# Attention stage: low halves of weights and queries, and the rotation's sum, moved from GpSimd to VectorE

## The chip, the cores and the metric

The kernel runs on one core of one Trainium2 chip. The core has a matrix engine (TensorE, PE in the profile; PEld is its weight load), three engines for elementwise work (VectorE or DVE, ScalarE or ACT, GpSimd or POOL), and a queue (SyncE, SP) that issues this kernel's DMAs. The metric is the device time of one execution in microseconds. Each engine takes its instructions strictly in the order of its own queue; semaphores between engines say when an instruction may start.

## The reference, cut to what matters

Two residual layers, 1024 tokens by 1024 channels, float32. The first has a recurrent mixer, the second windowed attention; each is followed by a squared-ReLU MLP. The attention mixer is:

```python
def rope(t, cos, sin):
    half = t.shape[-1] // 2
    t1, t2 = t[..., :half], t[..., half:]
    return jnp.concatenate([t1 * cos - t2 * sin, t2 * cos + t1 * sin], axis=-1)

def window_attention(u, w_qkv, sinks, w_o, cos, sin, band_mask):
    ...
    qkv = u @ w_qkv
    q, k, v = jnp.split(qkv, ...)          # 16 query heads, 4 key/value heads of 64
    q = rope(q..., cos, sin)
    k = rope(k..., cos, sin)
    ...                                    # blocks of 128 queries, keys of 3 blocks
    sc = einsum('bnqhgd,bnkhd->bnhgqk', qb, kb) * (HEAD_DIM ** -0.5)
    sc = where(band_mask, sc, -inf)
    p = softmax(concatenate([sc, sink], axis=-1), axis=-1)[..., :-1]
    o = einsum('bnhgqk,bnkhd->bnqhgd', p, vb)
    return o.reshape(bsz, s, N_Q_HEADS * HEAD_DIM) @ w_o
```

## The kernel before, in words

Products are made in a reduced float format (F32R). To keep accuracy each operand is split: the high half is a copy rounded to F32R by ACT (`split`, L85), the low half is the rest, source minus high half (L86). A product of two split operands takes three matmuls: high by high, high by low, low by high.

The attention stage works on slabs of 128 columns of `w_qkv`, each in two halves of 512 tokens. `load_split` brings a slab's weights from HBM into `raw`, and splits them into `w1hl`. `proj` (L116) makes the 24 matmuls of one half into PSUM tile `m`. The slab's `evac` then rotates: ACT copies PSUM to `qf` (L1130), four DMAs in SP's queue write the swapped 32-row groups to `rot` (L1132), DVE multiplies `qf` by the cosines in place (L1133), POOL multiplies `rot` by the sines (L1134), and their sum goes to `qf` (L1135). For queries (`put_q`) ACT copies 64 rows as the high half into one half of the tile `qst` (L1161), and the low half goes into the other 64 rows (L1162), so that one matmul contracts both. For keys (`put_k`) ACT makes `kh` (L1147), DVE `kl` (L1148), and DMAs copy both to the other 64 rows (L1149, L1150). Values (`do_v`) are transposed and split (L1178, L1179).

A unit is one of 4 key/value heads by one of 8 blocks of 128 queries: 32 units. For each of its 4 query heads it makes scores (PE L1208 on `kh`, L1209 on `kl`), adds the mask and takes the minimum of the negated scores (DVE L1210, tiles `sm` and `nm`), takes exponentials and their sum (ACT L1216), and the reciprocal (DVE L1217). Per block of keys it transposes (PE L1222), splits the probabilities into `ph` (ACT L85) and `pl` (DVE L86), and multiplies by the values (PE L1227, L1228). A transposed denominator (PE L1231), a sum (ACT L1233, DVE L1234) and a product (DVE L1237) end it. POOL also copies the sink's column into each `sm` (L1204).

The order in which slabs (K, Q, V, with group, slab and half) and units (U) are recorded is the string `ATT_ORDER`:

```python
ATT_ORDER = ("K00 Q010 Q000 K01 Q011 Q001 V00 !U00 !U01 !U02 V01 !U03 Q100 !U06 Q110 !U04 "
             "!U07 U05 Q101 !U11 !U12 !U10 !U13 Q111 Q200 U14 Q210 !U17 !U15 U16 Q201 Q211 "
             "K10 K11 V10 !U20 !U21 !U22 V11 !U23 Q300 Q310 !U24 !U26 !U27 !U32 !U33 !U30 "
             "!U25 Q301 Q311 !U31 !U34 !U35 !U36 U37")
```

This is not the queues' final order. A scheduler places all recorded instructions from its own estimate of what each takes on its engine, so an instruction that changes its engine can change the order on every engine. The slabs' matmuls, and near the end the first half of the output projection (L216), are what PE does between the steps of the units.

`mm_state['pool_lo']` is set when the first unit is recorded, and cleared at the stage's end. While it is set, a slab that is loaded has its weights' low half made by POOL, and the rotation's sum is POOL's too. The low halves of the queries are POOL's for the groups 1 to 3 (`G if g else V`). What the recurrent mixer, the MLPs and the output projections split is DVE's in any case.

Of the kernel before, what the change touches and what calls it, by code (L numbers as in the profile page):

```python
# [13 lines left out]
ALU = mybir.AluOpType  # L14
# [37 lines left out]
def trunk_kernel(ctx, tc, x, norm_g, rec_w_in, rec_conv_w, rec_conv_b, rg_w_r, rg_b_r, rg_w_i,  # L52
# [3 lines left out]
    V, A, G, T, Y = nc.vector, nc.scalar, nc.gpsimd, nc.tensor, nc.sync  # L56
# [11 lines left out]
    mm_state = {"n": 0, "att": False}  # L68
# [15 lines left out]
    def split(hi, lo, src, eng=None):  # L84
        A.activation(hi, src, AF.Copy)  # L85
        (eng or V).tensor_tensor(lo, src, hi, op=ALU.subtract)  # L86

    def load_split(dram_view, shape, pool, tag, bufs):
        raw = wp.tile(shape, F32, tag="raw", name="raw")
        Y.dma_start(raw, dram_view)  # L90
        both = pool.tile(shape[:1] + [2] + shape[1:], F32R, tag=tag, name=tag + "hl", bufs=bufs)
        hi, lo = both[:, 0], both[:, 1]
        split(hi, lo, raw, G if mm_state.get('pool_lo') else None)
        return hi, lo

    ahead = {}
# [1 line left out]
    def load_w1(w, c0):  # L98
        if (id(w.tensor), c0, w.offset) in ahead:
            return ahead.pop((id(w.tensor), c0, w.offset))  # L100
        return load_split(w[:, c0:c0 + P].rearrange("(k p) c -> p k c", p=P), [P, KT, P], wp, "w1", 3)
# [174 lines left out]
    def out_proj(ys, w, h_src, h_dst, layer, nxt, pre):  # L276
# [7 lines left out]
        def load_wo(k, pool, tag, bufs):  # L284
            return load_split(w[k * P:(k + 1) * P, :], [P, D], pool, tag, bufs)
# [820 lines left out]
    def attention(xt, a):  # L1106
        w_qkv = att_w_qkv[a]
        ys = [yp.tile([P, S], F32, tag="y", name=f"y{i}") for i in range(KT)]
        with phase("att") as pool:
# [13 lines left out]
            def h512(name, bufs=2):  # L1123
                return pool.tile([P, 512], F32, tag=name, name=name, bufs=bufs)

            def slab(c0, put):
                def evac(hf, o):
                    sl = slice(hf * 512, hf * 512 + 512)
                    qf, rot = h512("qf"), h512("rot", 2)
                    A.activation(qf, o, AF.Copy)  # L1130
                    for i, j in ((0, 1), (1, 0), (2, 3), (3, 2)):
                        Y.dma_start(rot[32 * i:32 * i + 32, :], qf[32 * j:32 * j + 32, :])  # L1132
                    V.tensor_tensor(qf, qf, cos[:, sl], op=ALU.mult)  # L1133
                    G.tensor_tensor(rot, rot, sin[:, sl], op=ALU.mult)  # L1134
                    (G if mm_state.get('pool_lo') else V).tensor_tensor(qf, qf, rot, op=ALU.add)  # L1135
                    put(hf, sl, qf)
                return load_w1(w_qkv, c0), evac

# [17 lines left out]
            def put_q(g, e0):  # L1156
                def f(hf, sl, r):
                    for e in range(2):
                        src, oth = (lo64, hi64) if e == 0 else (hi64, lo64)
                        t = qst[g, hf, e0 + e]  # L1160
                        A.activation(t[src, :], r[src, :], AF.Copy)  # L1161
                        (G if g else V).tensor_tensor(t[oth, :], r[src, :], t[src, :], op=ALU.subtract)  # L1162
                return f

            def do_v(pair):
# [85 lines left out]
            for st in ATT_ORDER.split():  # L1251
                if "U" in st:
                    g, n = int(st[-2]), int(st[-1])
# [101 lines left out]
```

## Time and profile before

| | |
|---|---|
| time, median of 3 runs | 2212.37 us (2211.07 to 2213.91) |
| profiled execution, its own time | 2211.91 us |
| its span, first to last instruction | 2210.2 us |
| mean granted clock of TensorE | 0.995 |
| instructions of POOL | 132, 168.8 us busy |
| of them, sums of the rotation on POOL (L1135) | 14, 19.7 us |
| low halves of queries on POOL (L1162) | 24, 31.5 us |
| low halves of weights on POOL (L86) | 8, 19.1 us |

Rows of instructions have: start and duration in us (or count, busy us and mean ns for a group), engine, source line, operation, output<-inputs, shapes; in square brackets, or behind the second bar, the idle time of the engine before them and what ended it. In the table of windows PE's busy time comes from modelled ends of pipelined matmuls. A granted clock of 1.00 is TensorE's full speed.

### The profile page before, as it was taken

The page shows a single profiled execution, that of the slowest core. Times are in us where ns is not written, and L with a number is a line of the kernel's source. Part 1 is how long each engine was busy: PE and PEld are TensorE (multiplying, and loading weights), DVE is VectorE, ACT ScalarE, POOL GpSimd, SP SyncE. Part 2 cuts the span into 40 slices and gives each one's busy share as a digit, 9 for nine tenths or more (in the row PEclk, how much of TensorE's full clock was granted, in tenths as well). Part 3 has the DMA queues.
Part 4 walks back from the last instruction along what each step waited for, and adds up shares of the span by engine and source line. Part 5 has one row for each costly group of instructions (what it writes and reads, how often), then busy time and mean ns, then how long its engine had stood idle before and what let it go on. Part 6 is the DMA issues. An engine that isn't in the chain of part 4 may idle for free.

```text
span 2210.2 us, 28051 instructions
## 1 busy us (share of the span) xinstructions
PE 2155.5 (98%) x10392; PEld 1779.2 (80%) x10392; DVE 1662.6 (75%) x2783; ACT 1145.7 (52%) x1798; POOL 168.8 (8%) x132
## 2 busy tenths in 40 slices
PE   8999999999999999999999999999999999999998
PEld 7878888787788888888888777777788888888886
DVE  6697867848976665778887775886896666578888
ACT  6576545635655446333444765775654455533332
POOL 0000000002000000000022245311200000000000
PEclk9999999999999999999999999999999999999999
DMA  5211111134444436444344112104354444634433
GB/s 144 62 34 58 29 30 39 39 124 138 143 156 154 152 135 254 153 149 157 115 143 129 44 38 63 39 25 140 128 170 156 148 151 159 228 133 152 157 122 131
DMA packets 180762, 260.88 MB, mean 118 GB/s; under 512 B 17040, under 2 KB 98960, under 8 KB 180624
## 3 DMA queue, kind: packets, MB, share of 16 engines
q1 hardware_dynamic: 180624, 259.07, 35.4%
q8 instruction: 82, 1.34, 0.3%
q14 instruction: 56, 0.46, 0.1%
HBM read 180.92 MB, written 70.78 MB: 114 GB/s over the span
## 4 chain that ended last, share of the span: by engine, by line
PE 78%; DVE 12%; ACT 6%; issue 2%; DMA 1%; POOL 1%; SPq 0%; DVEq 0%; ACTq 0%; POOLq 0%
PE m L437 15%; PE m L701 13%; PE m L116 12%; PE aux L437 10%; PE aux L701 10%; PE m L216 9%; PE aux L1227 1%; PE aux L1222 1%; DVE hb L267 1%; PE m L1208 1%; ACT sm L1216 1%; PE m L1209 1%; DVE acc L185 1%; PE aux L1049 1%; DVE w1hl L86 1%
## 5 line engine op out<-in xcount | busy, mean ns | idle before, releaser
L116 PE MATMUL m<-xh,w1hl 128*128 128x512 f32 (+1 forms) x1472 | 426.0, 369 | 0.2 <-ACT qf L1130 0.2
L116 PEld LDWEIGHTS m<-xh,w1hl 128*128 128x128 f32 x1472 | 266.3, 191 | 38.5 <-ACT qf L1130 0.4
L116 PE MATMUL m<-xl,w1hl 128*128 128x512 f32 (+1 forms) x736 | 271.5, 369 | 0.5 <-DVE xl L205 0.5
L86 DVE TENSOR_TENSOR w1hl<-raw,w1hl 128x1024 fp32r<-128x1024 f32 x110 | 133.8, 1219 | 89.7 <-ACT w1hl L85 89.4
L437 PE MATMUL m<-xh,ws 128*128 128x512 f32 x512 | 168.8, 392 | 4.1 <-ACT ws L85 3.0
L437 PE MATMUL aux<-xh,w1hl 128*128 128x512 f32 x512 | 168.7, 391 | 1.7 <-ACT u L453 1.3
L437 PE MATMUL m<-xh,w1hl 128*128 128x512 f32 x512 | 167.1, 389 | 0.0
L624 ACT ACTIVATE hidh<-hidl 128x1536 fp32r<-128x1536 f32 (+1 forms) x56 | 89.4, 1596 | 147.3 <-DMA hidl<-hs 147.3
L701 PE MATMUL m<-w2h,hidh 128*128 128x512 f32 x416 | 161.9, 389 | 0.0
L701 PE MATMUL m<-w2h,hidl 128*128 128x512 f32 x416 | 161.9, 389 | 0.0
L701 PE MATMUL m<-w2l,hidh 128*128 128x512 f32 x416 | 161.8, 389 | 0.0
L116 PEld LDWEIGHTS m<-xl,w1hl 128*128 128x128 f32 x736 | 140.8, 191 | 19.2 <-DVE xl L205 0.8
L265 POOL TENSOR_TENSOR mg<-acc,g 128x1024 f32<-128x1024 f32 x24 | 61.2, 2551 | 1162.6 <-DVE acc L610 608.0
L625 DVE TENSOR_TENSOR hidl<-hidl,hidh 128x1536 fp32r<-128x1536 f32 (+1 forms) x56 | 105.9, 1890 | 56.4 <-ACT hidh L624 56.4
L85 ACT ACTIVATE w1hl<-raw 128x1024 fp32r<-128x1024 f32 x118 | 124.1, 1055 | 33.9 <-DMA raw<-in_mlp_w_dram 9.6
L85 ACT ACTIVATE w2h<-b 128x1536 fp32r<-128x1536 f32 (+1 forms) x48 | 76.7, 1598 | 102.1 <-PE m L701 50.0
L85 ACT ACTIVATE ws<-s 128x512 fp32r<-128x512 f32 x88 | 55.3, 631 | 140.6 <-PE m L437 78.9
L701 PE MATMUL aux<-w2h,hidl 128*128 128x512 f32 x312 | 121.4, 389 | 0.0
L701 PE MATMUL aux<-w2h,hidh 128*128 128x512 f32 x312 | 121.4, 389 | 0.0
L701 PE MATMUL aux<-w2l,hidh 128*128 128x512 f32 x312 | 121.4, 389 | 0.0
L437 PEld LDWEIGHTS m<-xh,ws 128*128 128x128 f32 x512 | 95.8, 188 | 28.1 <-ACT ws L85 5.5
L437 PEld LDWEIGHTS aux<-xh,w1hl 128*128 128x128 f32 x512 | 96.1, 188 | 22.8 <-ACT u L453 2.3
(304 smaller groups left out, 4982.7 us busy)
## 6 DMA issues: line engine op xcount, KB each, us to landing
raw<-in_mlp_w_dram SPq DMA_DIRECT2D x32, 1024.0 KB, 5.6
hidl<-hs SPq DMA_DIRECT2D x42, 768.0 KB, 4.5
hs<-hid SPq DMA_DIRECT2D x104, 256.0 KB, 2.0
b<-in_mlp_w_dram SPq DMA_DIRECT2D x24, 768.0 KB, 4.8
raw<-in_rec_w_in_dram SPq DMA_DIRECT2D x28, 512.0 KB, 3.7
hidl<-hs SPq DMA_DIRECT2D x14, 1024.0 KB, 5.7
hs<-u SPq DMA_DIRECT2D x52, 256.0 KB, 2.0
hres<-hb SPq DMA_DIRECT2D x24, 512.0 KB, 2.7
```

What stands on the lines that cost most here:

```text
L85: A.activation(hi, src, AF.Copy)
L86: (eng or V).tensor_tensor(lo, src, hi, op=ALU.subtract)
L116: T.matmul(o[:, c0:c0 + nw], a[:, k, :], b[k // 4][half][:, k % 4, c0:c0 + nw], start=(n == 0), stop=(n == 3 * KT - 1))
L185: V.scalar_tensor_tensor(hg, hb, r[:, 0:1], g, op0=ALU.mult, op1=ALU.mult)
L216: T.matmul(o, p_[:, b * P:(b + 1) * P], q_[:, c * 512:(c + 1) * 512], start=(n == 0), stop=(n == n3 - 1))
L265: G.tensor_tensor(mg, m, g_post, op=ALU.mult)
L267: V.scalar_tensor_tensor(hb, mg, r[:, 0:1], hb, op0=ALU.mult, op1=ALU.add)
L437: T.matmul(o, a[:, k, :], b[:, k, :], start=(first and n == 0), stop=(n == 11), skip_group_check=not first)
L624: A.activation(h, f32(l), AF.Copy)
L625: V.tensor_tensor(l, f32(l), h, op=ALU.subtract)
L701: T.matmul(o, a_[:, j, sl], b_[:, j, :], start=(not more and n == 0), stop=(n == last), skip_group_check=more)
L1049: T.matmul(o, a_, b_, start=(i == 0), stop=(i == len(terms) - 1))
```

## The change

In three places DVE takes what POOL did: the low half of weights that are loaded while the units run, the sum that ends a rotation, and the low halves of the queries of groups 1 to 3. POOL keeps the sines' product (L1134) and the sinks' copies (L1204). The flag `pool_lo` is still set but no longer read.

```diff
@@ load_split
-        split(hi, lo, raw, G if mm_state.get('pool_lo') else None)
+        split(hi, lo, raw)
@@ slab, evac
                     V.tensor_tensor(qf, qf, cos[:, sl], op=ALU.mult)
                     G.tensor_tensor(rot, rot, sin[:, sl], op=ALU.mult)
-                    (G if mm_state.get('pool_lo') else V).tensor_tensor(qf, qf, rot, op=ALU.add)
+                    V.tensor_tensor(qf, qf, rot, op=ALU.add)
@@ put_q
                         A.activation(t[src, :], r[src, :], AF.Copy)
-                        (G if g else V).tensor_tensor(t[oth, :], r[src, :], t[src, :], op=ALU.subtract)
+                        V.tensor_tensor(t[oth, :], r[src, :], t[src, :], op=ALU.subtract)
```

The queues of PE, DVE, ACT and SP are reordered by it from the first unit to the end of the stage. Three places follow, as differences (- stood before, + stands now).

DVE's queue at the first unit, U00. `qst` are the queries of group 0, `m_10069` to `m_10081` the scores of its four heads:

```order
 L1133 TENSOR_TENSOR qf<-qf,cos 128x512
 L1135 TENSOR_TENSOR qf<-qf,rot 128x512
+L86 TENSOR_TENSOR w1hl<-raw,w1hl 128x1024
 L1162 TENSOR_TENSOR qst<-qf,qst 64x512 x2
 L1210 ISA sm,nm<-m_10069,mask,nsink 128x256
 L1210 ISA nm 128x1
+L1210 ISA sm,nm<-m_10073,mask,nsink 128x256
+L1210 ISA nm 128x1
```

A weight split now stands ahead of the two low halves that the first scores need.

POOL's queue where the last slabs of group 2 (`qf_11489`, `qf_11528`) and the second pair of keys (`qf_11576`, `qf_11619`) are rotated:

```order
-L1162 TENSOR_TENSOR qst_11461<-qf_11489,qst_11461 64x512
-L86 TENSOR_TENSOR w1hl_11991<-raw_11989,w1hl_11991 128x1024
 L1134 TENSOR_TENSOR rot_11529<-rot_11529,sin_9610 128x512
-L1135 TENSOR_TENSOR qf_11528<-qf_11528,rot_11529 128x512
-L1162 TENSOR_TENSOR qst_11462<-qf_11528,qst_11462 64x512
-L1162 TENSOR_TENSOR qst_11463<-qf_11528,qst_11463 64x512
 L1134 TENSOR_TENSOR rot_11577<-rot_11577,sin_9610 128x512
-L1135 TENSOR_TENSOR qf_11576<-qf_11576,rot_11577 128x512
-L86 TENSOR_TENSOR w1hl_12039<-raw_12037,w1hl_12039 128x1024
 L1134 TENSOR_TENSOR rot_11620<-rot_11620,sin_9610 128x512
-L1135 TENSOR_TENSOR qf_11619<-qf_11619,rot_11620 128x512
```

Between the sines' products nothing is left on POOL there.

DVE's queue at the same place, to the first score of the second pair's first unit:

```order
+L1162 TENSOR_TENSOR qst_11462<-qf_11528,qst_11462 64x512
+L1162 TENSOR_TENSOR qst_11463<-qf_11528,qst_11463 64x512
 L1133 TENSOR_TENSOR qf_11576<-qf_11576,cos_9609 128x512
+L1135 TENSOR_TENSOR qf_11576<-qf_11576,rot_11577 128x512
+L86 TENSOR_TENSOR w1hl_12039<-raw_12037,w1hl_12039 128x1024
 L1148 TENSOR_TENSOR kl_11543<-qf_11576,kh_11542 64x512
 L1148 TENSOR_TENSOR kl_11545<-qf_11576,kh_11544 64x512
+L1179 TENSOR_TENSOR vs_11637<-aux_11671,vs_11637 128x4x64
 L1210 ISA sm_11681,nm_11680<-m1_11683,mask_9613,nsink_9622 128x256
```

The keys' sum and a weight split now stand between their cosine product and their low halves.

## The prediction

> **What bounds the kernel now.** I read the head of the page first, then the chain that ended last, then the attention stage by windows, groups and waits.
>
> ```profile
> span 2210.2 us, 28051 instructions
> PE 2155.5 (98%) x10392; PEld 1779.2 (80%) x10392; DVE 1662.6 (75%) x2783; ACT 1145.7 (52%) x1798; POOL 168.8 (8%) x132
> ...
> 667.16 10.88 PE m L437 x48
> ```
>
> TensorE (PE) is the bound. The third row is one link of the chain: 48 matmuls of 512 columns in 10.88 us, 0.227 us each, with nothing between. Only what makes PE wait, or slows it, can move the end. The diff acts only after the first attention unit is recorded, so I look at the stretch from the attention stage's first products to the end of its last unit, about 1182 to 1510 us:
>
> ```profile
> core 0: us, PE busy (x) PEld busy (x) DVE busy (x) ACT busy (x) POOL busy (x), PEclk, DMA share, GB/s
> 1182.00:1510.00 328.00, 313.64 (x1705) 252.10 (x1704) 242.66 (x604) 213.25 (x482) 106.31 (x100) 0.98 0.17 47
> 1206.00:1212.00 6.00, 4.53 (x24) 4.27 (x25) 5.55 (x11) 3.30 (x8) 2.09 (x2) 0.72 0.66 184
> 1364.00:1376.00 12.00, 8.52 (x35) 6.88 (x35) 7.02 (x18) 5.84 (x17) 3.18 (x2) 0.72 0.36 99
> ```
>
> The columns are the busy times, then the granted clock. PE stands idle 328 - 313.64 = 14.4 us. In two places the clock falls (0.72 over 6 us and over 12 us), worth 0.28 x 6 = 1.7 and 0.28 x 12 = 3.4 us. Together 19.5 us: no gain can be larger, since the PE's own work does not change. Here are the first of the two places, and the second:
>
> ```profile
> 1204.04 2.37 POOL L86 TENSOR_TENSOR w1hl<-raw,w1hl 128x1024 fp32r<-128x1024 f32 x1 [0.82 <-ACT w1hl L85]
> 1204.64 4.00 DVE L1162 TENSOR_TENSOR qst<-qf,qst 64x512 fp32r<-64x512 f32 x2 [0.70 <-ACT qst L1161]
> 1206.36 1.73 POOL L1134 TENSOR_TENSOR rot<-rot,sin 128x512 f32<-128x512 f32 x1
> 1207.05 0.37 PE L1208 MATMUL m<-kh,qst 128*128 128x256 f32 x1 [1.80 <-POOL w1hl L86]
> 1208.69 0.58 PE L1208 MATMUL m<-kh,qst 128*128 128x256 f32 x1 [0.42 <-DVE qst L1162]
> ...
> 1356.55 1.99 DMA rot<-qf
> ...
> 1360.92 1.30 POOL L1134 TENSOR_TENSOR rot<-rot,sin 128x512 f32<-128x512 f32 x1
> 1362.30 1.29 POOL L1135 TENSOR_TENSOR qf<-qf,rot 128x512 f32<-128x512 f32 x1
> 1363.55 2.36 POOL L86 TENSOR_TENSOR w1hl<-raw,w1hl 128x1024 fp32r<-128x1024 f32 x1
> ...
> 1364.29 2.17 DVE kl L1148
> ...
> 1366.62 0.47 PE L1208 MATMUL m<-kh,qst 128*128 128x256 f32 x2 [2.18 <-DMA kh<-kh]
> 1368.85 0.77 PE L1209 MATMUL m<-kl,qst 128*128 128x256 f32 x2 [1.29 <-DMA kl<-kl]
> ```
>
> At 1204 two low halves of queries on DVE take 4.00 us instead of about 1.4, because they lie beside POOL's weight split and then beside its sines' product, and the first scores wait for them. At 1364 the keys of the second pair are late: their rotation stood in POOL's queue behind another slab's work, and their low half on DVE took 2.17 us beside POOL's split of 1363.55. Each place cost the wait, and the lower clock behind it.
>
> **The change, part by part.** The groups that it moves, and their like on DVE:
>
> ```profile
> L1162 POOL TENSOR_TENSOR qst<-qf,qst 64x512 fp32r<-64x512 f32 x24 | 31.5, 1311 | 18.6 <-ACT qst L1161 17.8
> L1135 POOL TENSOR_TENSOR qf<-qf,rot 128x512 f32<-128x512 f32 x14 | 19.7, 1410 | 11.7 <-DVE qf L1133 11.3
> L86 POOL TENSOR_TENSOR w1hl<-raw,w1hl 128x1024 fp32r<-128x1024 f32 x8 | 19.1, 2382 | 28.5 <-DVE y L1237 14.6 <-ACT w1hl L85 13.8
> ...
> L86 DVE TENSOR_TENSOR pl<-aux,ph 128x512 fp32r<-128x512 f32 x88 | 60.0, 687 | 18.5 <-ACT ph L85 18.1
> L1133 DVE TENSOR_TENSOR qf<-qf,cos 128x512 f32<-128x512 f32 x20 | 18.3, 914 | 10.5 <-POOL w1hl L86 5.2 <-DMA rot<-qf 5.0
> L1162 DVE TENSOR_TENSOR qst<-qf,qst 64x512 fp32r<-64x512 f32 x8 | 8.1, 1010 | 1.6 <-ACT qst L1161 1.4
> L86 DVE TENSOR_TENSOR w1hl<-raw,w1hl 128x1024 fp32r<-128x1024 f32 x4 | 4.9, 1226 | 0.5 <-ACT w1hl L85 0.3
> ```
>
> POOL loses 24 + 14 + 8 instructions, 70.3 us. DVE gets the same 46: 24 x 0.687 + 14 x 0.687 + 8 x 1.226 = 35.9 us. It sheds some stretching: its low halves of queries mean 1010 against the 687 of the same 512 columns read from PSUM, 8 x 0.32 = 2.6 us, and part of L1133's 20 x 0.23 = 4.5 us. So DVE goes from 242.7 to about 274 of 328 us, 74 to 83%. No DMA is added or dropped, PE and ACT do the same work. No instruction of POOL is now a link between a slab's cosine product and its finished query, except the sines' product (L1134), which stays.
>
> (1) The first scores, 1204 to 1210. In the new DVE queue the weight split (1.23) stands ahead of the two low halves: from 1204.04, where POOL's began, it lasts to 1205.3, then come 2 x 0.69 and one sines' product of 1.29 that can slip between: 1206.7 to 1208.0 against 1204.64 + 4.00 = 1208.64 now. PE has five more projection matmuls of 256 columns ahead of the first score, at half of 0.227 each 0.6 us of cover. Saved: 0.6 to 2.0 us of wait, and 0 to 1.7 of clock. I take 1.8.
>
> (2) The keys, 1356 to 1376. The transfer landed at 1356.55 + 1.99 = 1358.54, the sines' product began at 1360.92. With POOL's queue empty it begins 2.4 us sooner, the sum is 0.6 shorter, and the low half 1.5; the weight split that the new queue puts ahead of it costs about 0.6 back. The high half comes 3.0 us sooner (wait now 2.18), the low half 3.9 (the two waits 3.47). Bounds: all of 3.47 + 3.4 = 6.9, or nothing, if the transfers from `qf` land late. I take 5.5.
>
> (3) Waits in the rest of the stage that POOL ends:
>
> ```profile
> ACT qst L1161 <- POOL qf L1135: 8.1, 7, 2.5
> ...
> PE m L1208 <- POOL qst L1162: 1.0, 2, 0.6
> ...
> 1300.00:1310.00 10.00, 8.59 (x44) 6.08 (x43) 6.09 (x13) 6.49 (x14) 8.06 (x6) 1.00 0.21 61
> 1380.00:1390.00 10.00, 9.33 (x49) 7.93 (x50) 9.31 (x27) 6.87 (x16) 0.19 (x1) 1.00 0.23 54
> 1410.00:1420.00 10.00, 9.89 (x57) 7.96 (x56) 9.08 (x24) 8.32 (x17) 5.78 (x5) 1.00 0.10 26
> 1450.00:1460.00 10.00, 7.94 (x42) 5.35 (x41) 8.12 (x24) 8.09 (x19) 4.93 (x6) 1.00 0.01 2
> ```
>
> PE's own wait of 1.0 goes. ACT waits 8.1 us for POOL's sums, and in its queue the copies and exponentials that PE needs stand behind. Where POOL is busy 8.06 and 4.93 of 10 us, PE is idle 1.41 and 2.06; I take 3.0 of these 3.5, with nothing and 7 as the ends. So 4.0.
>
> (4) DVE's load. The rows of 1380 and 1410 show DVE 93 and 91% busy with PE idle only 0.67 and 0.11: a DVE near nine tenths does not by itself stop PE. But the new order heaps the work up. Two stretches of the present run, from a unit's first score reduction to another's (units 8 to 15, and 20 to 31 of 0 to 31):
>
> ```profile
> 1274.40:1332.30 57.90, 55.77 (x296) 43.25 (x297) 43.76 (x123) 39.63 (x97) 25.48 (x24) 1.00 0.14 37
> 1396.30:1495.30 99.00, 94.94 (x501) 73.94 (x501) 81.13 (x204) 70.70 (x162) 25.75 (x28) 1.00 0.10 27
> ```
>
> In the first the new DVE queue holds 5 sums, 9 low halves, 2 weight splits and one cosine product more, and 3 short products less: 15 x 0.69 + 2 x 1.23 - 0.8 = 12.0, so 55.8 us. PE has 12 projection matmuls more and two others less, 2.3 us: 60.2 us at unchanged waits, DVE 93% busy, as much as its fullest row. I add 2. In the second DVE gets 4 sums and 8 low halves and drops some small work, less 1.4 of stretching: 89 us. PE has 19 projection matmuls, 6 value products and 16 transposes fewer, 7.5 us, which come elsewhere: 91.5 us at unchanged waits. At 93% DVE takes 89/0.93 = 95.7: I add 4. Ends: nothing, and 15 if DVE reaches only 87%.
>
> (5) The sines' product no longer queues behind other work on POOL, but DVE now waits for it in its own queue, where the sum stands right behind the cosine product: score reductions and probabilities' low halves queue behind it. A wait of at most 1.29 each, 14 times; most of it is the stretch of L1133 that exists already. I count 0 and put it with (4).
>
> Sum: -1.8 - 5.5 - 4.0 + 6 = -5.3 us. The profiled execution took 2211.9 us (span 2210.2), 0.5 under the median of 2212.37; I take the sum from the median: 2207.
>
> **Two rules weighed.** The rows: two low halves with both inputs in SBUF took 4.00 us beside POOL, while L86's `pl`, which reads PSUM, keeps a mean of 687 in the same stage. The Trainium skill, "SBUF — State Buffer", "Who interferes with whom", says that a DVE instruction with two SBUF inputs and a POOL instruction that reads SBUF exclude each other for the whole instruction. The trace agrees. It speaks against the change too: the 46 instructions brought to DVE are all of that kind, and the sines' products that stay on POOL can hold each of them up. That is the last rival below.
>
> The rows: the clock fell after PE waits of 1.80 and 2.18 us. The Trainium skill, "TensorE: Matmul & The Clock Gate", Part 1, has the clock halved after an idle window of about 3.4 us. By that rule shorter waits would not explain the drops, and their removal would leave the clock's share, 0.9 of (1) and about 3 of (2): the sum would be about -1.4, 2211. The trace differs, and I go by the trace.
>
> **The rivals.** *DVE becomes the bound.* For it: the two stretches of (4), 93 and 97% demand. Against: the rows of 1380 and 1410. If DVE reaches only 87% there, the cost is 4 + 10.5 = 14.5 instead of 6; against it the gains of (1) to (3), some of which a late DVE also takes, say 8 of 11.3: 2219. It decides from about 16 us of cost on for slower by over 0.2%, or 12 with half the gains.
>
> *Given back.* The keys' wait is shortened but PE then waits at another unit, because the new order spends its projections earlier (12 more by unit 15) and has fewer to cover the later units: gains of 8, cost of 7: 2211. At the same time of 2211 would come out that the waits go and the clock still drops, from some other idle time of PE; the two drops, each right behind a long wait, speak against it.
>
> *DVE absorbs all.* No cost in (4), and (1) to (3) near their ends: 3 + 6 + 5 = 14: 2198. The rows of 1380 and 1410 speak for it, the heaps of (4) against it.
>
> *The exclusion moves to the sines' product.* 14 products of 1.29 us, if each holds up a DVE instruction that PE's work waits for: at most 18 us less the 4.5 of today, on top of the forecast at half weight: 2214, at full weight 2220.
>
> **How the numbers follow.** 0.2% of 2212 is 4.4 us, about what a measurement of this kernel can tell from no change. Forecast (faster by about 5, own range 2200 to 2208): 0.36. DVE absorbs all: 0.11. Given back, or the forecast with a little more cost: 0.26, and clock drops that stay: 0.04. DVE the bound: 0.17. The exclusion: 0.06. Faster 0.47, same 0.30, slower 0.23. The range, 2199 to 2218, takes in the forecast and giving back, most of the slower cases and half of the faster rival.
>
> **What would show it.** L1162, L1135 and L86 `w1hl` stand under DVE alone, near 690, 690 and 1230 ns, POOL is busy about 106.3 - 70.3 = 36 us in the stage, and L1162's mean comes down from 1010. No clock drop near the keys of the second pair, and no wait of PE for them over 1 us. ACT waits no more for POOL's sums, but for DVE's. DVE near 83% of the stage. It is wrong if DVE stands over 95% for tens of microseconds with PE's waits on `nm`, `ph` and `pl` grown, if the keys still come late, or if a new wait of PE near 2 us brings a clock drop of its own.

## The result and the profile after

The changed kernel takes 2201.43 us (median of 4 runs, 2200.35 to 2202.96), the kernel before 2212.93 beside it: a ratio of 0.9947, 95% interval 0.9935 to 0.9958, so 11.7 us faster (9.3 to 14.4). The profiled execution took 2201.63 us. From here on "idle" is a window's length less PE's busy time in it.

The head of the page, for the changed kernel:

```profile
span 2199.9 us, 28012 instructions
PE 2150.0 (98%) x10392; PEld 1777.1 (81%) x10392; DVE 1687.2 (77%) x2829; ACT 1145.3 (52%) x1798; POOL 101.0 (5%) x86
```

PE does the same 10392 matmuls. The span fell by 10.3 us: PE's busy time by 2155.5 - 2150.0 = 5.5 (it is shorter where the clock does not fall), the idle rest by 4.8. The stage in three pieces by windows, first the kernel before, then the changed one (length, then busy time of PE, PEld, DVE, ACT, POOL, then the granted clock, the DMA share and GB/s):

```profile
1182.00:1420.00 238.00, 227.60 (x1254) 185.75 (x1253) 170.49 (x423) 150.99 (x337) 87.07 (x79) 0.98 0.21 56
1420.00:1470.00 50.00, 46.39 (x248) 35.51 (x246) 43.01 (x108) 36.09 (x85) 18.67 (x18) 1.00 0.15 43
1470.00:1500.00 30.00, 29.65 (x158) 23.15 (x157) 22.79 (x57) 21.84 (x53) 0.57 (x3) 1.00 0.00 1
```

```profile
1182.00:1420.00 238.00, 234.64 (x1313) 191.77 (x1312) 201.66 (x485) 160.35 (x360) 33.10 (x45) 0.99 0.21 57
1420.00:1470.00 50.00, 45.36 (x235) 35.25 (x235) 44.12 (x113) 35.82 (x86) 5.01 (x7) 1.00 0.15 40
1470.00:1500.00 30.00, 29.84 (x157) 23.22 (x156) 24.64 (x59) 18.63 (x38) 0.39 (x2) 1.00 0.18 59
```

Up to 1420 the idle time falls from 10.40 to 3.36 us, while DVE rises from 170.5 to 201.7 of 238. From 1420 to 1470, which I call the tail, it rises from 3.61 to 4.64. The gain is made in the long first piece, and a little is given back in the tail. The two places of the prediction, now by the timeline:

```profile
1203.96 1.23 DVE L86 TENSOR_TENSOR w1hl<-raw,w1hl 128x1024 fp32r<-128x1024 f32 x1 [1.69 <-ACT w1hl L85]
1204.20 2.12 POOL L1134 TENSOR_TENSOR rot<-rot,sin 128x512 f32<-128x512 f32 x1 [2.65 <-DMA rot<-qf]
1205.22 2.37 DVE L1162 TENSOR_TENSOR qst<-qf,qst 64x512 fp32r<-64x512 f32 x2
1206.97 0.36 PE L1208 MATMUL m<-kh,qst 128*128 128x256 f32 x1 [1.14 <-POOL rot L1134]
...
1354.09 0.69 DVE L1135 TENSOR_TENSOR qf<-qf,rot 128x512 f32<-128x512 f32 x1 [1.20 <-POOL rot L1134]
1354.76 1.23 DVE L86 TENSOR_TENSOR w1hl<-raw,w1hl 128x1024 fp32r<-128x1024 f32 x1
1355.90 1.40 DVE L1148 TENSOR_TENSOR kl<-qf,kh 64x512 fp32r<-64x512 f32 x2
```

At the first scores the exclusion is still there: the sines' product takes 2.12 us beside the split, and the two low halves 2.37. (The wait is named after POOL, which was done at 1204.20 + 2.12 = 1206.32; PE started when the first of DVE's two low halves was done.) PE waits 1.14 us in place of 1.80 + 0.42, and the clock stays up. The second pair's keys are split at 1355.9, not at 1364.3, and PE has no wait for them. Windows of the changed kernel (the first two are its units 8 to 15 and 20 to 31, the stretches of the prediction's term (4)), then a group of DVE, and waits:

```profile
1274.60:1331.90 57.30, 56.97 (x305) 45.46 (x304) 53.38 (x135) 41.84 (x100) 7.98 (x12) 1.00 0.16 42
1383.30:1480.00 96.70, 90.97 (x484) 71.39 (x484) 86.19 (x218) 70.03 (x161) 9.69 (x15) 1.00 0.11 28
...
1280.00:1290.00 10.00, 9.89 (x59) 7.88 (x58) 9.58 (x27) 8.44 (x18) 0.38 (x2) 1.00 0.22 64
1290.00:1300.00 10.00, 9.92 (x55) 8.03 (x54) 9.76 (x22) 5.89 (x15) 1.47 (x2) 1.00 0.26 67
...
L1162 DVE TENSOR_TENSOR qst<-qf,qst 64x512 fp32r<-64x512 f32 x32 | 23.4, 730 | 2.1 <-ACT qst L1161 1.3
...
ACT qst L1161 <- DVE qf L1135: 1.4, 2, 0.9
PE m L216 <- DVE xhl L86: 2.2, 1, 2.2
```

From 1280 to 1300 DVE is 96 and 98% busy, and PE is idle 0.11 and 0.08 us in each ten. ACT's wait for the sums shrank from 8.1 to 1.4 us. What is new is PE's wait of 2.2 us in the tail, for a low half of the output projection's weights that DVE made late.

### The profile page after: what moved, and what is told of

Same layout as the page of the kernel before. It is cut to its first block, busy times and chain, and to the rows that moved or that the text cites. A ratio compares the mean times of both kernels' runs of the same rounds, so it can differ in the third digit from the quotient of the medians.

```text
span 2199.9 us, 28012 instructions
## 1 busy us (share of the span) xinstructions
PE 2150.0 (98%) x10392; PEld 1777.1 (81%) x10392; DVE 1687.2 (77%) x2829; ACT 1145.3 (52%) x1798; POOL 101.0 (5%) x86
## 3 DMA queue, kind: packets, MB, share of 16 engines
q8 instruction: 82, 1.34, 0.3%
## 4 chain that ended last, share of the span: by engine, by line
PE 79%; DVE 12%; ACT 5%; issue 2%; DMA 2%; POOL 0%; SPq 0%; DVEq 0%; ACTq 0%; POOLq 0%
PE m L437 15%; PE m L116 14%; PE m L701 13%; PE aux L437 10%; PE aux L701 10%; PE m L216 9%; PE aux L1222 1%; PE aux L1227 1%; DVE hb L267 1%; PE m L1208 1%; DVE w1hl L86 1%; PE m L1209 1%; DVE acc L185 1%; PE aux L1228 1%; PE aux L1049 1%
## 5 line engine op out<-in xcount | busy, mean ns | idle before, releaser
L86 DVE TENSOR_TENSOR w1hl<-raw,w1hl 128x1024 fp32r<-128x1024 f32 x118 | 143.6, 1219 | 92.7 <-ACT w1hl L85 92.5
```

## The experiments

The kernel before took 2213.2 to 2214.0 us beside these runs, so they are compared by their ratio to it. In microseconds of 2213 the changed kernel stands at -11.7 (-14.4 to -9.3).

**One part alone**, on the kernel before:

```diff
# e1_weights, L93
-        split(hi, lo, raw, G if mm_state.get('pool_lo') else None)
+        split(hi, lo, raw)
# e2_queries, L1162
-                        (G if g else V).tensor_tensor(t[oth, :], ...
+                        V.tensor_tensor(t[oth, :], ...
# e3_sum, L1135
-                    (G if mm_state.get('pool_lo') else V).tensor_tensor(qf, qf, rot, op=ALU.add)
+                    V.tensor_tensor(qf, qf, rot, op=ALU.add)
```

> The kernel before with one part of the change: only the low halves of the weights (8 of 128x1024) go from POOL to DVE. Theory A (links on POOL came late, and POOL's long instructions stretched DVE's): the split of 2.38 us no longer lies beside the keys' low half (2.17 us) nor beside the queries' low halves at 1204 (4.00 us), so both waits of PE shrink and at least one of the two periods at half clock goes: 4 to 6 us faster, 2207 to 2209. Theory B (it is the new order of the queues that did it, not the engine): the part alone gives any value, and the three parts alone do not add up to 11.5. Theory C (DVE is near its bound, and its load eats part of each gain): 8 x 1.22 = 9.8 us more DVE, 0 to 2 us faster.

> The kernel before with only the low halves of the queries (24 of 64x512) moved from POOL to DVE. Theory A: POOL loses 31.5 us, its sums and sines' products queue behind fewer instructions, ACT's 8.1 us of waiting for POOL's sums shrink by half; the first scores (1204) are not touched, since group 0's low halves were on DVE already: 2 to 4 us faster, 2208 to 2210. Theory B: any value within 5 us of before on both sides. Theory C: 24 x 0.69 = 16.5 us more DVE, the largest of the three loads: no gain or 1 to 4 us slower.

> The kernel before with only the rotation's sum (14 of 128x512) moved from POOL to DVE. Theory A: the sum takes 0.69 instead of 1.41 us and no longer queues on POOL, but DVE's sum waits for POOL's sines' product, which still queues behind POOL's weights and queries: 1 to 3 us faster, 2209 to 2211, with a keys' wait of PE near 1368 still over 1 us. Theory B: any value within 5 us of before on both sides. Theory C: 9.7 us more DVE, 0 to 2 us faster.

Weights: 0.9981 (0.9972 to 0.9990), -4.2 us. Queries: 1.0004 (0.9996 to 1.0013). Sum: 0.9998 (0.9989 to 1.0007). The first is where the theory of POOL's links (A) put it; the other two give nothing, against its 1 to 4 us, and that is what the theory of DVE's load (C) allowed. Together they make about 4 of the 11.7. Rows of each, weights (timeline), queries (waits up to 1420, then the tail's window), then sum (timeline):

```profile
1357.08 2.98 POOL L1162 TENSOR_TENSOR qst<-qf,qst 64x512 fp32r<-64x512 f32 x2 [0.74 <-ACT qst L1161]
1357.59 1.33 DVE L1133 TENSOR_TENSOR qf<-qf,cos 128x512 f32<-128x512 f32 x1 [3.77 <-DMA rot<-qf]
...
1360.14 1.29 POOL L1134 TENSOR_TENSOR rot<-rot,sin 128x512 f32<-128x512 f32 x1
...
1365.83 0.35 PE L1208 MATMUL m<-kh,qst 128*128 128x256 f32 x1 [2.46 <-DMA kh<-kh]
```

```profile
PE m L1208 <- POOL w1hl L86: 1.8, 1, 1.8
PE m L1208 <- DMA kh<-kh: 1.7, 1, 1.7
...
1420.00:1470.00 50.00, 43.27 (x230) 33.25 (x229) 44.69 (x114) 34.88 (x83) 8.21 (x11) 1.00 0.15 43
```

```profile
1415.15 0.44 PE L1208 MATMUL m<-kh,qst 128*128 128x384 f32 x1 [1.83 <-POOL qst L1162]
```

Each leaves another link. With the weights moved, PE waits 1.1 us at the first scores in place of 2.2, and the clock stays up there; but the keys are still late: their transfer is there at 1357.59, but the sines' product stands behind two low halves of queries on POOL until 1360.14, and PE waits 2.46 us. With the queries moved, PE still waits 1.8 us at the first scores, where POOL splits weights, and 1.7 us for the second pair's keys, and the tail is idle for 6.73 us with DVE at 89%. With the sum moved, a score waits 1.83 us for POOL's low half of a query.

**One part left on POOL**, on the changed kernel (the same three lines, one of them back):

> The changed kernel with the low halves of the weights (8 of 128x1024) back on POOL; queries and sums stay on DVE. The three parts alone gave -4.2, 0 and 0 us against -11.5 together. Theory A (any kind of link left on POOL holds up the others, so the gain comes only when all three are gone): the waits of 1.96 and 0.97 us at the first scores come back with a split of 2.38 us beside them, and the keys of the second pair are late again: 6 to 9 us slower than the changed kernel, 2207 to 2210. Theory B (the changed kernel's order happens to be a lucky one): the time is unrelated to which part is left, anything from 2201 to 2214. Theory C (DVE's load decides): 9.8 us less DVE, 0 to 3 us faster than the changed kernel.

> The changed kernel with the low halves of the queries of groups 1 to 3 (24 of 64x512) back on POOL; weights and sums stay on DVE. Theory A: PE waits for POOL's low halves before the scores near 1415 and 1430, as it did when only the sum was moved (2.00, 0.67, 1.68 and 0.67 us): 4 to 6 us slower than the changed kernel, 2205 to 2208. Theory B: anything from 2201 to 2214. Theory C: 16.5 us less DVE, 1 to 4 us faster than the changed kernel.

> The changed kernel with the rotation's sum (14 of 128x512) back on POOL; weights and queries stay on DVE. Theory A: the sum costs 1.41 instead of 0.69 us but queues behind nothing but sines' products, and ACT and DVE wait for it a little longer: 1 to 4 us slower than the changed kernel, 2202 to 2206. Theory B: anything from 2201 to 2214. Theory C: 9.7 us less DVE, 0 to 3 us faster than the changed kernel.

Weights left: 0.9995 (0.9987 to 1.0004), -1.1 us, so nearly the whole gain is lost, more than expected. Queries left: 0.9964 (0.9951 to 0.9978), -8.0. Sum left: 0.9971 (0.9961 to 0.9982), -6.4, a loss of 5.3 against 1 to 4 expected. Theory C is out for all three: less load on DVE made none of them faster than the changed kernel. With the weights left, the timeline shows how (the first three rows from one place, the next three from the keys of the second pair):

```profile
1344.66 2.39 POOL L86 TENSOR_TENSOR w1hl<-raw,w1hl 128x1024 fp32r<-128x1024 f32 x1 [5.49 <-PE aux L1222]
1345.28 2.32 DVE L1162 TENSOR_TENSOR qst<-qf,qst 64x512 fp32r<-64x512 f32 x1
1348.37 0.50 PE L1228 MATMUL aux<-pl,vs 128*128 128x512 f32 x1 [1.23 <-DVE pl L86]
...
1360.24 2.39 POOL L86 TENSOR_TENSOR w1hl<-raw,w1hl 128x1024 fp32r<-128x1024 f32 x1
1360.31 2.87 DVE L1135 TENSOR_TENSOR qf<-qf,rot 128x512 f32<-128x512 f32 x1 [1.19 <-POOL rot L1134]
1367.56 0.39 PE L1208 MATMUL m<-kh,qst 128*128 128x256 f32 x1 [1.22 <-DMA kh<-kh]
```

A single low half of 64x512 takes 2.32 us beside POOL's split, and a sum 2.87, against means of 730 and 684 in the changed kernel. PE's work stands behind them. The waits at the first scores are back too (1.79 and 0.81 us), and the clock falls there and at the keys (0.89 over 1200 to 1215 and 0.94 over 1350 to 1380; 0.89 and 0.89 in the kernel before). With the sum left on POOL, its timeline shows the chain that the prediction's third term is about:

```profile
1322.13 1.28 POOL L1135 TENSOR_TENSOR qf<-qf,rot 128x512 f32<-128x512 f32 x1 [0.69 <-DVE den L1217]
1323.45 1.28 ACT L1161 ACTIVATE qst<-qf 64x512 fp32r<-64x512 f32 x2 [1.49 <-POOL qf L1135]
1324.75 1.09 ACT L85 ACTIVATE ph<-aux 128x512 fp32r<-128x512 f32 x2
1325.40 0.50 PE L1227 MATMUL aux<-ph,vs 128*128 128x512 f32 x1 [1.29 <-ACT ph L85]
```

ACT stands still 1.49 us for POOL's sum, the probabilities' high half behind it is late, and PE waits 1.29. With the queries left, the time came out as expected but the mechanism did not: the waits for POOL's low halves near 1415 and 1430 did not come back (0.3 us in all up to 1420). PE is idle 4.40 us up to 1420 against 3.36, and 5.80 in the tail against 4.64, of which 3.6 are waits for ACT. That is 2.2 us more; the profiled execution took 2203.38 us, the fastest of five (median 2206.01), so the rest of the loss is not located:

```profile
1182.00:1420.00 238.00, 233.60 (x1302) 191.99 (x1301) 190.04 (x460) 156.40 (x351) 59.23 (x65) 1.00 0.22 59
1420.00:1470.00 50.00, 44.20 (x230) 33.11 (x229) 39.19 (x106) 34.87 (x82) 8.03 (x11) 1.00 0.09 27
PE aux L1227 <- ACT ph L85: 3.6, 6, 1.0
```

**Reads on POOL that nobody waits for**, on the changed kernel. It is the one run here in which PE, DVE, ACT and SP have the same instructions in the same order as in the changed kernel:

```diff
                     put(hf, sl, qf)
+                    if mm_state.get('pool_lo'):
+                        for d in range(2):
+                            G.tensor_tensor(rot, rot, sin[:, sl], op=ALU.mult)
```

> The changed kernel with two more products on POOL behind each rotation's sum (28 of 128x512, both inputs in SBUF, about 1.4 us each, 39 us in all) whose result nobody reads; the order of PE's and DVE's queues stays that of the changed kernel. If POOL's instructions cost by standing beside DVE's (exclusion): DVE's instructions with two inputs in SBUF stretch (mean of L1133 and L1162 from 730 back to 900 or more), and on a DVE that is 95 to 99% busy that shows: 4 to 8 us slower than the changed kernel, 2205 to 2209. If POOL's instructions cost only as links that others wait for: nobody waits for these but POOL's own sines' products, 0 to 2 us slower, 2201 to 2203, and the same PE waits as in the changed kernel.

0.9957 (0.9945 to 0.9970), -9.5 us: 2.2 us slower than the changed kernel by the two centres, with intervals that overlap. The groups (lines stand three further down in this kernel):

```profile
L1139 POOL TENSOR_TENSOR rot<-rot,sin 128x512 f32<-128x512 f32 x28 | 42.2, 1508 | 31.9 <-DVE qf L1135 27.7 <-DVE den L1220 3.2
L1165 DVE TENSOR_TENSOR qst<-qf,qst 64x512 fp32r<-64x512 f32 x32 | 28.0, 876 | 2.1 <-ACT qst L1164 1.3
L1151 DVE TENSOR_TENSOR kl<-qf,kh 64x512 fp32r<-64x512 f32 x8 | 7.5, 943 | 0.9 <-ACT kh L1150 0.7
```

The stretching is there: low halves of queries 730 to 876 ns, 32 x 0.146 = 4.7 us in all, and of keys to 943. But with 42 us of POOL beside it, it costs about 2 us, and at most some 8 by the outer ends of the two intervals; in the profile PE is idle 5.13 us up to 1420 against 3.36, and the clock falls once in the tail (0.97 over its 50 us, 1.7 us). So POOL's products of 1.4 us cost little where nobody waits for them; both readings in the expectation were half right.

**The sines' product on DVE too**, on the changed kernel, and the same with the low halves of four rows of output weights and four of the output projection's inputs on POOL:

```diff
# e4_sines and e11_sines_wo, L1134
-                    G.tensor_tensor(rot, rot, sin[:, sl], op=ALU.mult)
+                    V.tensor_tensor(rot, rot, sin[:, sl], op=ALU.mult)
# e11_sines_wo and e7_wo_hid (load_split hands eng on to split)
-            split(*hid[k], ys[k])
+            split(*hid[k], ys[k], G if layer % 2 and k < 4 else None)
...
-            return load_split(w[k * P:(k + 1) * P, :], [P, D], pool, tag, bufs)
+            return load_split(w[k * P:(k + 1) * P, :], [P, D], pool, tag, bufs, G if layer % 2 and k < 4 else None)
```

> The changed kernel with the sines' product (20 of 128x512) on DVE too, so that POOL does almost nothing in the stage. If what is left of exclusion with POOL still costs (20 products of 1.48 us): L1133 falls from 728 to about 690 ns, L1134 takes 690, PE's wait for the rotated tile at the first scores (1.30 us) goes: 1 to 3 us faster than the changed kernel, 2198 to 2200. If DVE is near its bound (theory C): 20 x 0.69 = 13.8 us more on an engine that is 95 to 99% busy for windows of 10 us: 4 to 10 us slower than the changed kernel, 2205 to 2211. If only the order counts (theory B): any value from 2197 to 2211.

> The sines' product on DVE too, as in the run that took 2210.7 us, and the output projection's low halves (8 of 128x1024) on POOL as in the run beside this one. That run lost least up to 1420 (PE lost 16.6 us from 1180 to 1420, against 19.1 in the changed kernel) and then 17.2 us from 1420 to 1460, where its projections had run out. If DVE's load at the end of the stage made that tail: DVE sheds 4.9 us or more there, the tail falls by 4 to 8 us, 2202 to 2206. If the tail comes from projections spent too early, with PE waiting on the chain of exponentials and low halves of probabilities: it stays within 3 us, 2208 to 2213.

> The changed kernel with the low halves of the first four rows of output weights and of the first four inputs of the output projection (8 of 128x1024, made at the end of the stage and just behind it) on POOL, which is idle there. Theory A: what is left to gain is at 1430 to 1450, where PE waits 0.95 and 2.33 us for DVE's low halves of these; on POOL they take about 2.4 instead of 1.2 us, but nothing stands ahead of them: the two waits go, 2 to 4 us faster than the changed kernel, 2198 to 2200. Rival: POOL's 2.4 us come as late as DVE's queue, or stretch DVE's low halves beside them: no change within 2 us.

Sines on DVE: 0.9988 (0.9979 to 0.9997), -2.7 us. With the output projection's halves on POOL as well: 0.9946 (0.9932 to 0.9959), -12.0, the changed kernel's time. Windows of the first, then the tail of the second:

```profile
1182.00:1420.00 238.00, 235.35 (x1323) 195.36 (x1321) 209.24 (x502) 159.94 (x364) 5.79 (x26) 1.00 0.21 57
1420.00:1470.00 50.00, 40.47 (x198) 28.69 (x199) 44.21 (x112) 30.71 (x75) 1.27 (x6) 0.97 0.12 37
```

```profile
1420.00:1470.00 50.00, 45.27 (x231) 35.20 (x230) 42.53 (x113) 34.61 (x83) 3.92 (x7) 0.97 0.07 23
```

With POOL almost empty the first piece is the best of all, 2.65 us idle at 88% DVE; the tail is then idle 9.53 us. Taking low halves off DVE brings the tail to 4.73, and the time, 2201.1 us, went below the 2202 to 2206 expected if DVE's load made the tail. But the order of the queues moved too, so that the output projection's weights are split sooner and its products can fill PE; the two are not told apart, so that DVE's load made the tail is likely and not shown.

The output projection's halves on POOL without the sines' product on DVE: 0.9961 (0.9948 to 0.9973), -8.6 us, no gain over the changed kernel and about 3 us behind it by the centres. The tail improves, 3.24 us idle against 4.64, but up to 1420 PE is idle 7.64 us against 3.36: the splits were ordered earlier, where they lie beside DVE's work. Its timeline:

```profile
1374.88 2.38 POOL L86 TENSOR_TENSOR w1hl<-raw,w1hl 128x1024 fp32r<-128x1024 f32 x1 [2.12 <-ACT w1hl L85]
1375.01 2.79 DVE L1148 TENSOR_TENSOR kl<-qf,kh 64x512 fp32r<-64x512 f32 x1
1378.59 0.50 PE L1228 MATMUL aux<-pl,vs 128*128 128x512 f32 x1 [1.92 <-DVE pl L86]
```

One low half of 0.68 us takes 2.79, and PE waits 1.92 for what stands behind it. So the rival of the expectation has the mechanism, stretched low halves, but not the size: it allowed 2 us.

**Doses of DVE**: products as in the diff of the reads above, on `V` instead of `G`, one or two behind each rotation's sum.

> The changed kernel with one more product on DVE behind each rotation's sum (14 of 128x512, about 0.69 us each, 9.6 us in all) whose result nobody reads. It doses the load that the change gave DVE (46 instructions). If DVE's slack holds (the links that left POOL were the gain, and DVE's load cost next to nothing): 0 to 3 us slower than the changed kernel, 2201 to 2205, PE's losses grown at 1420 to 1460 only. If DVE is at its bound: most of the 9.6 us shows, 6 to 10 us slower, 2207 to 2212, with PE's waits grown all over the stage.

> The same with two products more behind each rotation's sum, 28 in all, 19.3 us. If DVE's slack holds for the first dose but not beyond: 5 to 10 us slower than the changed kernel, 2207 to 2212. If DVE is at its bound already: 14 to 19 us slower, 2216 to 2221. If DVE has slack everywhere: under 4 us.

One: 1.0011 (1.0002 to 1.0020), +2.4 us. Two: 1.0060 (1.0047 to 1.0072), +13.3. Against the changed kernel that is 14 us for 9.6 us of added DVE time, and 25 for 19.3: more than any reading in the expectations allowed. Where the first dose shows, by its windows, then the second by its first piece and one row of the timeline:

```profile
1260.00:1340.00 80.00, 79.39 (x418) 62.81 (x417) 75.14 (x185) 55.27 (x130) 11.01 (x17) 1.00 0.16 44
...
1420.00:1470.00 50.00, 41.00 (x184) 29.33 (x183) 44.01 (x111) 31.04 (x75) 2.78 (x6) 0.90 0.07 21
```

```profile
1182.00:1420.00 238.00, 225.70 (x1247) 184.51 (x1247) 202.51 (x481) 151.13 (x345) 30.30 (x42) 0.98 0.21 56
...
1354.79 1.22 PE L116 MATMUL m<-xh,w1hl 128*128 128x512 f32 x2 [5.90 <-DVE w1hl L86]
```

In the first, PE is idle for 0.61 of the 80 us between 1260 and 1340, with DVE 94% busy. The tail pays most: 9.00 us idle against 4.64, and a clock of 0.90 over 50 us, worth 5, which is 9.4 of the 15.3 us by which the span is longer. The second dose pays earlier: 12.30 us idle up to 1420, and 5.90 of them are one wait for the low half of a slab's weights, which DVE made late. The last projection product starts at 1422.6 us with one dose (1423.8 in the changed kernel, 1414.9 with the sines' product on DVE, 1435.6 with two doses). As I read it, PE has other work while the projections last, so that a late DVE costs little, and it pays when they run out, or when DVE is so late that the projections' own weights are not there. That the dear part begins at their end is shown in the first three and not in the last; the reason is not tested by itself.

## Why the prediction was right, and which terms were off

The direction was right, and so was the way to it; the gain was twice the forecast (11.7 by the runs against 5.3), nearer the 14 of the rival in which DVE absorbs all, to which the prediction gave a chance of 0.11.

- Term (1), first scores, -1.8: the wait fell from 2.22 to 1.14 and the clock drop went (1.7), so -2.8. The new order of weight split and low halves was as predicted, and the stretching between DVE and the sines' product stayed, as bounded.
- Term (2), the keys, -5.5: both waits and the clock drop gone, -6.9, the upper bound. The 0.6 held back for the weight split ahead of the low half was covered.
- Terms (3) and (4), -4.0 and +6. Idle time up to 1420 fell by 7.04, of which (1) and (2) are 1.08 + 3.47; the rest is -2.5. From 1420 to 1500 it rose by 1.03 - 0.19 = 0.8. Together -1.7 where the prediction had +2. The mechanism of (3) is shown by the run with the sum left on POOL, and by ACT's wait of 8.1 falling to 1.4.
- The step that failed is (4): the price of 2 + 4 us for DVE at 93%. In the first of its stretches DVE was 93% busy as forecast, and PE's idle time fell from 2.13 to 0.33 us where the prediction added 2; in the second, with DVE at 89%, it rose from 4.06 to 5.73, by 1.7 where the prediction added 4 (its 89 us of DVE there are 1 more than its own terms give, 81.1 + 12 x 0.69 - 1.4 = 88.0). Its rule, that DVE can be no busier than its fullest row of before, took a row that happened to be there for a ceiling; from 1280 to 1300 DVE was 96 and 98% busy.
- Term (5), 0: DVE waited 4.8 us for the sines' product in all. With the sines' product on DVE the first piece is 0.7 us less idle; so near 0, as said.

These add to -11.4; the profiled execution pays 1.7 back (last section), which makes -9.7 of the 10.3 by which its span fell.

The rival "DVE becomes the bound" was wrong for this kernel and right 10 us further on. It was priced as an average over two stretches; with one dose most of the bill comes in the tail, with two it comes before it as well. Of the signs of being wrong, DVE over 95% came for twenty microseconds, with next to no wait of PE; a new wait near 2 us came in the tail, without a drop of the clock.

The three parts do not add. Alone they give 4.2, -0.9 and 0.4 us; left out of the whole they cost 10.6, 3.7 and 5.3. Of three links on one slow engine the others hide the gain of each, and the weight splits, the longest, hide most. That is how I read it; that the parts do not add was also what the theory of the order (B) said. How much of each single figure is the order of the queues, which is planned anew in every version but the one with POOL's reads, is not settled: the run with the queries left shows that a time can come out as expected for another reason.

## What to carry to other kernels

Judge a helper engine by what stands behind its instructions: here 68 us less of POOL (168.8 to 101.0) for 25 us more of an already busy DVE (1662.6 to 1687.2) gave 11.7 us, since ACT and PE no longer waited for POOL, and its long instructions no longer held up DVE's. Move links that feed one another together, and do not judge each by itself. Here an engine at 93 to 98% cost nothing while the bound engine had other work to fill with; look for the price where that filler runs out, and where the filler itself needs the busy engine, as with two doses.

## What was not expected of the hardware

POOL's effect on a single DVE instruction grows with the length of POOL's instruction. Splits of 128x1024 (2.4 us) made DVE instructions of 0.68 us last 2.3 to 2.9; in the run with 28 further products of 1.5 us, none of DVE's sums and low halves of 512 columns took more than 1.80. In all, the two stretched DVE alike: its groups L1133, L1135, L1148 and L1162 take 57.6 us in the changed kernel, 64.4 with 19 us of weight splits on POOL, and 64.7 with 42 us of further products. The kernel with the splits lost 10.6 us and the one with the products about 2, so that what stands behind a stretched instruction counts for more than the sum. With the sines' product on DVE and POOL almost empty, the four groups have means of 678 to 686 ns. The Trainium skill, "SBUF — State Buffer", "Who interferes with whom", says that the ports which the two share are under an exclusive lock and that the order of issue decides which of them blocks; by that the longest hold is the length of POOL's longest instruction, and the trace agrees (2.79 us of DVE beside a split of 2.38).

The clock fell to half behind a wait of about 2.2 us ahead of this stage in the changed kernel, and not in the profile of before, where the same wait stands. The timelines, before and then after, and the window of 1180 to 1186 of each:

```profile
1181.40 1.07 PE L191 MATMUL aux<-ident,acc 128*128 128x128 f32 x8 [2.18 <-DVE r L152]
...
1180.00:1186.00 6.00, 4.60 (x39) 4.48 (x40) 5.37 (x9) 3.16 (x6) 1.01 (x2) 1.00 0.37 106
```

```profile
1180.31 1.06 PE L191 MATMUL aux<-ident,acc 128*128 128x128 f32 x8 [2.19 <-DVE r L152]
...
1180.00:1186.00 6.00, 5.69 (x36) 5.58 (x37) 4.39 (x8) 3.17 (x6) 1.02 (x2) 0.72 0.52 165
```

The clock of 0.72 over 6 us costs 1.7. The drop stands in the profiles of all twelve experiments too (0.83 over 1177 to 1187, and 1.00 in before's), so the exception is before's profiled execution. In the tail of the changed kernel a wait of 2.17 us brought no drop. So a wait near 2 us may or may not halve the clock, and its length alone does not tell. The Trainium skill, "TensorE: Matmul & The Clock Gate", Part 1, calls the window in which activity is watched free-running, so that the point of a change depends on where in the window the work falls; that fits one wait with a drop in one execution and without in another. The clock records of the traces bear it out: in each of the fourteen, the changes of the clock lie whole multiples of 3.413 us apart. Cut into such slots, the changed kernel's wait ahead of the stage lies whole in one (2.19 us idle of 3.41), and the clock is halved for the next; before's falls into two (0.73 and 1.45), as does the wait of 2.17 in the tail (1.30 and 0.87). How much idle time in a slot is enough stays open: 1.34 us was followed by a drop in one run, 1.89 by none in another. That part of the Trainium skill has the clock halved after an idle window of about 3.4 us, longer than any of these waits, and there the trace differs.
